# The last 256 gate and 256 up features of a feed-forward block as one more unit of seven block products, and its first two units taken by turns

## The chip, the cores and the metric

The kernel runs on one core of one Trainium2 chip. The metric is the device time of one launch in microseconds (us); smaller is better. Before the change the median of three runs is 862.22 us (861.01 to 862.43). One execution was also recorded by the hardware profiler, and everything below that is read from a view is read from that execution.

## The reference, cut to what matters

One encoder layer: two mixers, a cross-attention over a memory, and a feed-forward block (SwiGLU), on 512 tokens with 1024 features. The change is in the last block, and begins where the cross-attention ends:

```
h = h + memory_cross_attention(rms_norm(h, xattn_norm_g[i]), memn, w_q[i], w_k[i], w_v[i], w_xo[i])
h = h + swiglu(rms_norm(h, ffn_norm_g[i]), w_gate[i], w_up[i], w_down[i])
...
def swiglu(hn, w_gate, w_up, w_down):
    return (jax.nn.silu(hn @ w_gate) * (hn @ w_up)) @ w_down
```

`hn` is 512 x 1024, `w_gate` and `w_up` are 1024 x 2816, `w_down` is 2816 x 1024, all float32.

## The kernel before, in words

**Float32 from two halves.** TensorE is fed with operands that are split in two: `split` (line 83) casts a tile to a rounded half on ScalarE (line 85, "hi") and subtracts that from the tile on VectorE (line 86, "lo"). Each product of two such operands is three matmuls: hi by hi, hi by lo, lo by hi. So each block of weights that arrives from memory costs one cast on ScalarE and one subtraction on VectorE before TensorE may use it. The halves of weights live in three buffers each (`hi`, `lo`, line 108); a fourth block can be split only when the oldest of the three has been multiplied. Some blocks have a place of their own instead (`sums_place`, line 131: `s1`, `s2`, `s4`).

**Units of seven products.** 512 columns of `w_gate` or `w_up` are a unit. Its matrix product (two halves of the 1024 input features, two halves of the tokens, two halves of the columns) is done by Strassen's method in Winograd's form: seven block products in place of eight. They have the numbers 1, 2, 5, 6, 7, 4, 3 in the order of use. `product` (line 1252) does one: 24 matmuls with 256 moving columns. The weight side of 1, 2, 7 and 3 starts from blocks that are loaded as they are (tiles `b11`, `b21`, `b22`); that of 5, 6, 7 and 4 needs sums of blocks: `t` is loaded and a second block is added onto it by an accumulating DMA that GpSimd issues (line 193), and three further sums for each unit are made on VectorE (line 200). `plan_unit` (line 173) lists for each product its loads, how many products ahead each load is asked for (4 for `b11` and `b21`, 7 for `t`, 5 for the add onto `t` and for `b22`), and the making of its halves. `t`, `b21` and `b22` have two buffers each. The token side needs operands of its own: 1 and 2 take the tokens 0 to 255 as they are, 7 and 4 the tokens 256 to 511 or a difference, 5, 6 and 3 sums of both (`sum1`, `sum2`, `sum4`, lines 1729 to 1740).

**The last 512 columns are not a unit.** 2816 is five times 512 and 256 more. The last 256 columns of `w_gate` and of `w_up` (from `FS`, line 340) are multiplied in the ordinary way: `gate_part` (line 1767) and `feat` (line 1784), each 96 matmuls of 256 moving columns, thus four times the 24 of a product, eight for both. They go first, mixed with products 1 and 2 of the first unit, because the tokens 256 to 511 come out of the cross-attention and its norm later than the tokens 0 to 255 (`last_blocks`, line 1682; `turn_row`, line 1668). One matmul of 512 columns (`idle_product`, line 1265) writes to nothing that is read. Their results are `pair`: the gate part through SiLU on ScalarE (line 1717), then multiplied by the up part on VectorE (line 1720).

**What sets the order.** `plan` is the list of all blocks of weights in the order of their use. `next_w` (line 351) hands out the next one, asks for the loads that are due, and writes the splits of the next two blocks into the program. The program order is a priority only: a scheduler orders each engine's queue by it among what it takes to be ready, so that work written later stands earlier in a queue where nothing else was ready. `keep_in_program_order` and `behind` (line 117) pin single instructions. The queues are worked in that order on the chip. The copies and adds that prepare `w_down` (`plan_sums`, line 276) are hung on entries of the plan by their number, every fourth from entry 122 on (line 348): a copy that SyncE issues (line 293), and an accumulating DMA that GpSimd issues (line 294).

**Around it.** `unit_start` (1745) does product 1 and copies it, `unit_second` (1758) adds product 2 to the copy; the loop over the units is at line 1832, and in it products 1 and 2 of the next unit stand between the products of the present one.

Of the kernel before, what the change touches and what calls it, by code (L numbers as in the profile page):

```python
# [17 lines left out]
P = 128  # L18
# [34 lines left out]
def hybrid_layer_kernel(  # L53
# [29 lines left out]
    def split(dst_hi, dst_lo, src):  # L83

        hi = nc.scalar.copy(dst_hi, src)  # L85
        lo = nc.vector.tensor_tensor(dst_lo, src, dst_hi.bitcast(F32), ALU.subtract)  # L86
        if pinned[0]:
            in_order(hi)
            in_order(lo)
        return hi  # L90


    pinned = [False]
# [79 lines left out]
    def plan_unit(w, c0, ordered=False):  # L173

        kh = KD // 2
        b = lambda i, j: block(w, i * kh, kh, c0 + 256 * j, 256)
# [25 lines left out]
        def make(nm, *then):  # L202
# [6 lines left out]

        return {q: ((w, c0, q), loads, made) for q, loads, made in (  # L210
            (1, [(4, plain("b11", b(0, 0)))], make("b11")),
# [34 lines left out]
    def plan_units(units, down):  # L246


        made = [plan_unit(*u, ordered=i < 2) for i, u in enumerate(units)]
        for i in range(2):  # L250
            plan_block(w_gate, 4 * i, 4, FS, 256, place=i + 1, ordered=True,
                       then=None if i else lambda ins: behind(ins, xo_cast[0]))
            plan.append(made[0][i + 1])
        plan_feat(w_up, FS, KD)
        for i, m in enumerate(made):
# [85 lines left out]
    UNITS = [(w, c0) for c0 in range(0, FS, 512) for w in (w_gate, w_up)]  # L341
# [923 lines left out]
    def idle_product(x, y):  # L1265

        in_order(nc.tensor.matmul(aux("idle", (P, 2, 256)), x[:, 0, 0:P], y, start=True, stop=True))

# [372 lines left out]
    for wi in range(2):  # L1641
        held.append((wi,) + next_w(w_xo, 2 * wi, 2, 0, 512))
        for t in range(NT):
            out_rows(wi, t)
            tick(1.3)
            between.get((wi, t), lambda: None)()
    held += [(wi,) + next_w(w_xo, 2 * wi, 2, 0, 512) for wi in (2, 3)]
# [20 lines left out]
    def turn_row(t, turned=False):  # L1668
        to_feat(scaled.pop(t), fn_hi, fn_lo, slice(t * P, (t + 1) * P), full, turned=turned, copied=True)
# [46 lines left out]
    def gate_evac(m, j, ps):  # L1716
        nc.scalar.activation(pair[:, j, :], ps, AF.Silu)

    def up_evac(m, j, ps):
        nc.vector.tensor_tensor(pair[:, j, :], pair[:, j, :], ps, ALU.mult)  # L1720


    a11, a12, a21, a22 = full[:, K0, T0], full[:, K1, T0], full[:, K0, T1], full[:, K1, T1]
# [5 lines left out]
    def sum1():  # L1729
        V.tensor_tensor(a22, a21, a22, ALU.subtract)  # L1730
        make_op(5, 1, a22)

    def sum2():
        V.tensor_tensor(s3, a11, a21, ALU.subtract)
        V.tensor_tensor(a11, a22, a11, ALU.subtract)
        make_op(6, 2, a11)

    def sum4():
        V.tensor_tensor(a12, a12, a11, ALU.add)
        make_op(3, 4, a12)  # L1740

    fn_q = lambda ks, ts: (fn_hi[:, ks, ts], fn_lo[:, ks, ts])
    ops = {1: fn_q(K0, T0), 2: fn_q(K1, T0), 7: fn_q(K0, T1), 4: fn_q(K1, T1)}
# [7 lines left out]
    def put(u, f, ts, src):  # L1751
        dst = acts(u[1] // 512, f)[:, :, ts]
        if u[0] is w_gate:
            nc.scalar.activation(dst, src, AF.Silu)
# [6 lines left out]

    ps = [bank("pf0"), bank("pf1")]
    ws = []

    def gate_part(i, ts):
        if ts is T0:
            ws.append((4 * i,) + next_w(w_gate, 4 * i, 4, FS, 256))
        feat_block(ps, ws[i], fn, KD, 4, ts, ts is T0)  # L1770
        tick(2.7)

    gate_part(0, T0)
    begun = unit_start(UNITS[0])
    gate_part(1, T0)
    idle_product(ops[1][0], fn_hi[:, 4:6, T0])
    unit_second(UNITS[0], begun[1])
    for i in range(2):
        gate_part(i, T1)
    for j in range(2):  # L1780
        gate_evac(FS // P + j, j, ps[j])
    sum1()
    later(1, sum2)
    feat(w_up, FS, fn, KD, up_evac, parts=2, ps=[aux("pf0"), aux("pf1")])
# [246 lines left out]
```

## Time and profile before

| | |
|---|---|
| median of three runs | 862.22 us (861.01 to 862.43) |
| the profiled execution: span from first to last instruction (the page gives no other time for it) | 859.5 us |
| TensorE busy | 852.2 us |
| VectorE busy | 663.7 us |
| ScalarE busy | 465.9 us |
| GpSimd busy | 86.2 us |
| moved by DMA | 170.61 MB, mean 198 GB/s |

Times in the views are us from the start of the span. PE is TensorE, PEld its loading of the stationary operand, DVE is VectorE, ACT is ScalarE, POOL is GpSimd, SP is SyncE; a "q" behind a name is the issuing of DMAs. In the timeline a line has its start, its length, engine, program line, operation, output and inputs, and in square brackets the time for which the engine had been idle and what ended that. In the chain of waits a line has the start, the time it adds to the chain, engine, output, line and number of instructions.

### The profile page before, as it was taken

Reading aid. Unit: us, or ns where it says so; the run is one execution under the profiler, and the core shown is the slowest. Engines: PE = TensorE matmul, PEld = TensorE weight load, DVE = VectorE, ACT = ScalarE, POOL = GpSimd, SP = SyncE. Lnnn points to the kernel's source line nnn. Section 1 sums busy time; section 2 is a strip of 40 time slices with the busy share of each in tenths; the row PEclk is TensorE's granted clock in tenths of the full one; section 3 lists DMA queues with packets and bytes.
Section 4 is the critical chain, followed back from the end, with each engine's and each line's share of the span. In section 5 each row is a group of like instructions: output and inputs, shape, how many; then the busy total and the mean of one; then the engine's idle time right before and its main releaser. Section 6 shows DMA issues by size and latency. Waiting matters only on the chain.

```text
span 859.5 us, 14730 instructions
## 1 busy us (share of the span) xinstructions
PE 852.2 (99%) x5760; PEld 764.1 (89%) x5760; DVE 663.7 (77%) x1078; ACT 465.9 (54%) x698; POOL 86.2 (10%) x119
## 2 busy tenths in 40 slices
PE   9999999999999999999999999999999999999997
PEld 6888888888889988899899888999999999988886
DVE  7898898899646867678758656767877768899776
ACT  7834953244455534457557444645545554655674
POOL 0002101211021111010010001010211111000000
PEclk9999999999999999999999999999999999999999
DMA  9869666888575798635696555557899898366664
GB/s 270 229 229 252 143 171 160 227 212 203 138 221 162 250 321 260 213 110 196 215 275 169 133 152 143 147 176 180 206 242 234 209 230 219 96 186 203 200 192 164
DMA packets 116200, 170.61 MB, mean 198 GB/s; under 512 B 9489, under 2 KB 80801, under 8 KB 116002
## 3 DMA queue, kind: packets, MB, share of 16 engines
q1 hardware_dynamic: 95778, 140.51, 50.8%
q0 software_dynamic: 20064, 28.55, 20.3%
q8 instruction: 45, 0.74, 0.3%
q10 hardware_dynamic: 288, 0.61, 0.2%
q14 instruction: 25, 0.20, 0.1%
HBM read 160.75 MB, written 48.73 MB: 244 GB/s over the span
## 4 chain that ended last, share of the span: by engine, by line
PE 98%; DMA 1%; ACT 0%; SPq 0%; DVE 0%; issue 0%
PE pf L379 27%; PE pt L379 17%; PE px L1261 13%; PE pq L1261 6%; PE dx L379 5%; PE dq L379 5%; PE pv L1261 3%; PE bx L1261 3%; PE qx L1261 3%; PE dv L379 2%; PE pz L968 2%; PE qv L1261 1%; PE po L379 1%; PE psc L379 1%; PE py L1025 1%; PE qq L1261 1%
## 5 line engine op out<-in xcount | busy, mean ns | idle before, releaser
L85 ACT CAST whi<-wraw 128x1024 fp32r<-128x1024 f32 x141 | 145.3, 1031 | 161.4 <-PE pf L379 61.0
L86 DVE TENSOR_TENSOR wlo<-wraw,whi 128x1024 fp32r<-128x1024 f32 x141 | 168.2, 1195 | 55.5 <-ACT whi L85 54.8
L379 PE MATMUL pf<-xn,whi 128*128 128x512 f32 x448 | 139.4, 392 | 0.0
L379 PEld LDWEIGHTS pf<-xn,whi 128*128 128x128 f32 x448 | 83.4, 188 | 16.9 <-issue 0.2
L379 PE MATMUL pf<-xn,wlo 128*128 128x512 f32 x224 | 87.7, 392 | 0.0
L1261 PE MATMUL px<-fn,whi 128*128 128x256 f32 x480 | 83.5, 277 | 0.0
L1261 PEld LDWEIGHTS px<-fn,whi 128*128 128x128 f32 x480 | 72.5, 188 | 0.2
L86 DVE TENSOR_TENSOR wlo<-b,whi 128x1024 fp32r<-128x1024 f32 x40 | 48.9, 1223 | 26.0 <-ACT whi L85 26.0
L85 ACT CAST whi<-b 128x1024 fp32r<-128x1024 f32 x40 | 42.2, 1054 | 47.8 <-PE px L1261 27.8
L1261 PE MATMUL px<-fn,wlo 128*128 128x256 f32 x240 | 66.4, 277 | 0.0
L1261 PE MATMUL pq<-s,whi 128*128 128x256 f32 x320 | 55.0, 276 | 0.0
L86 DVE TENSOR_TENSOR wlo<-t,whi 128x1024 fp32r<-128x1024 f32 x30 | 36.7, 1225 | 19.4 <-ACT whi L85 19.4
L85 ACT CAST whi<-t 128x1024 fp32r<-128x1024 f32 x30 | 31.6, 1054 | 36.1 <-PE pv L1261 13.4
L379 PEld LDWEIGHTS pf<-xn,wlo 128*128 128x128 f32 x224 | 42.0, 188 | 8.9 <-issue 0.2
L1261 PEld LDWEIGHTS pq<-s,whi 128*128 128x128 f32 x320 | 48.1, 188 | 0.0
L1261 PEld LDWEIGHTS px<-fn,wlo 128*128 128x128 f32 x240 | 45.1, 188 | 0.0
L1261 PE MATMUL pq<-s,wlo 128*128 128x256 f32 x160 | 44.2, 276 | 0.0
L379 PE MATMUL pt<-whi,xn 128*128 128x512 f32 x128 | 43.4, 404 | 0.0
L379 PE MATMUL dx<-whi,s 128*128 128x512 f32 x132 | 41.4, 390 | 0.0
L379 PE MATMUL dq<-whi,s 128*128 128x512 f32 x122 | 38.1, 389 | 0.0
L294 POOL DMA_DIRECT2D dsum<-in_w_down_dram x12 | 13.3, 1105 | 170.4 <-DMA dsum<-in_w_down_dram 166.2
L1261 PEld LDWEIGHTS pq<-s,wlo 128*128 128x128 f32 x160 | 30.1, 188 | 0.0
(456 smaller groups left out, 2221.7 us busy)
## 6 DMA issues: line engine op xcount, KB each, us to landing
wraw<-in_w_in_dram SPq DMA_DIRECT2D x34, 512.0 KB, 5.2
dsum<-in_w_down_dram SPq DMA_DIRECT2D x20, 512.0 KB, 6.3
wraw<-dsum SPq DMA_DIRECT2D x20, 512.0 KB, 4.3
b<-in_w_gate_dram SPq DMA_DIRECT2D x15, 512.0 KB, 5.2
b<-in_w_up_dram SPq DMA_DIRECT2D x15, 512.0 KB, 5.4
wraw<-in_w_down_dram SPq DMA_DIRECT2D x15, 512.0 KB, 4.6
dsum<-in_w_down_dram POOLq DMA_DIRECT2D x10, 512.0 KB, 7.9
dsum<-dsum POOLq DMA_DIRECT2D x10, 512.0 KB, 7.9
```

The lines of the kernel that those rows point to most:

```text
L85: hi = nc.scalar.copy(dst_hi, src)
L86: lo = nc.vector.tensor_tensor(dst_lo, src, dst_hi.bitcast(F32), ALU.subtract)
L294: plan[j + step][1].append((0, lambda d=dst, x=more: nc.gpsimd.dma_start(d, x, accum_op=ALU.add)))
L379: m = nc.tensor.matmul(ps, a[x], b[y], start=start and i == 0, stop=stop and i == 2, skip_group_check=free)
L968: nc.tensor.matmul(ps[:, g, :], wt[:, g, :], u[:, o * GO + g, :], start=True, stop=True)
L1025: in_order(nc.tensor.matmul(ps[64 * j:64 * j + 64, :, :, h, :].rearrange("p q d c -> p d q c"), a, b, start=k == ks[0], stop=k == ks[2], t ...
L1261: nc.tensor.matmul(ps[:, j, :], a[x], b[y], start=start and j == k == i == 0, stop=k == 3 and i == 2, skip_group_check=True)
```

## The change

The 256 last columns of `w_gate` and the 256 last of `w_up` become one unit, number 0: its first half of columns is the gate part, its second the up part, done with the same seven products as the others. It has its results put into `pair`. The eight products' worth of ordinary matmuls and the idle matmul go.

The first stretch is now a list written out by hand, `LEAD`: a pair is (unit, product). Units 0 and 1 go by turns; products 1 and 2 of unit 2 stand among them. The ordinary loop starts with product 5 of unit 2. The token operands are made at other places: rows 256 to 511 are only copied to `full` when they have been transposed (`turn_row`), the operand of product 5 is made from them in two parts (`fifth_part`), then those of 6 (`sixth`), 7 (first `split_last`), 3 (`third`) and 4 (second `split_last`). A SiLU of one column (`ready`) is put at an earlier place, in the cross-attention's last stage. Units 0 to 2 have their loads in program order, before it was units 0 and 1. The diff, without the plain removal of `sum1`, `sum2`, `sum4`, `gate_evac`, `up_evac`, `gate_part` and `idle_product`:

```diff
-    def plan_unit(w, c0, ordered=False):
+    def plan_unit(w, c0, ordered=False, place=None):
...
-        b = lambda i, j: block(w, i * kh, kh, c0 + 256 * j, 256)
+        b = lambda i, j: block(w, i * kh, kh, c0 + 256 * j, 256) if c0 < FS or j == 0 else block(w_up, i * kh, kh, c0, 256)
...
+        def first():
+            ops = halves(r["b11"], place)
+            if place is not None:
+                behind(cast[0], xo_cast[0])
+            return ops
...
-            (1, [(4, plain("b11", b(0, 0)))], make("b11")),
+            (1, [(4, plain("b11", b(0, 0)))], first),
...
-        made = [plan_unit(*u, ordered=i < 2) for i, u in enumerate(units)]
-        for i in range(2):
-            plan_block(w_gate, 4 * i, 4, FS, 256, place=i + 1, ordered=True,
-                       then=None if i else lambda ins: behind(ins, xo_cast[0]))
-            plan.append(made[0][i + 1])
-        plan_feat(w_up, FS, KD)
-        for i, m in enumerate(made):
+        made = [plan_unit(*u, ordered=i < 3, place=None if i else 1) for i, u in enumerate(units)]
+        plan.extend(made[n][q] for n, q in LEAD)
+        for i, m in list(enumerate(made))[2:]:
...
-    UNITS = [(w, c0) for c0 in range(0, FS, 512) for w in (w_gate, w_up)]
+    UNITS = [(w_gate, FS)] + [(w, c0) for c0 in range(0, FS, 512) for w in (w_gate, w_up)]
+    LEAD = ((0, 1), (1, 1), (0, 2), (1, 2), (2, 1), (0, 5), (1, 5), (0, 6), (1, 6), (0, 7), (1, 7), (0, 4), (0, 3), (1, 4),
+            (2, 2), (1, 3))
...
+    ready = np_.tile([P, 1], F32, tag="ms", name="ready", bufs=2)
+    behind(nc.scalar.activation(ready, mhalf, AF.Silu), halved[0][0])
...
     def turn_row(t, turned=False):
-        to_feat(scaled.pop(t), fn_hi, fn_lo, slice(t * P, (t + 1) * P), full, turned=turned, copied=True)
+        if t < 2:
+            to_feat(scaled.pop(t), fn_hi, fn_lo, slice(t * P, (t + 1) * P), full, turned=turned, copied=True)
+            return
+        xs = scaled.pop(t)
+        for q in range(2):
+            ps = aux("ptr", (P, 4, P))
+            for j in range(4):
+                k = 4 * q + j
+                nc.tensor.transpose(ps[:, j, :], xs[:, k * P:(k + 1) * P], ident)
+            nc.scalar.copy(full[:, 4 * q:4 * q + 4, t * P:(t + 1) * P], ps)
...
+    def fifth_part(t):
+        if 5 not in ops:
+            ops[5] = sums_place(1, 4, 256, APART)
+        r = slice((t - 2) * P, (t - 1) * P)
+        V.tensor_tensor(s3[:, :, r], a21[:, :, r], a22[:, :, r], ALU.subtract)
+        split(ops[5][0][:, :, r], ops[5][1][:, :, r], s3[:, :, r])
+        fifth.extend(halved[0])
+        if t == 3:
+            behind(silus[0], fifth[-2])
+
+    def sixth():
+        V.tensor_tensor(a21, a11, a21, ALU.subtract)
+        behind(V.tensor_tensor(a11, s3, a11, ALU.subtract), fifth[-1])
         make_op(6, 2, a11)
+    def third():
         V.tensor_tensor(a12, a12, a11, ALU.add)
         make_op(3, 4, a12)
...
+    def lead_product(n, q):
+        u, d = UNITS[n], lead.setdefault(n, {})
+        if q == 1:
+            d["x"], d["v"] = unit_start(u)
+        elif q == 2:
+            unit_second(u, d["v"])
+        elif q == 5:
+            d["q"] = aux("pq").rearrange("p (j t) -> p j t", j=2)
+            product(d["q"], u, 5, True, ops)
+        elif q == 6:
+            product(d["x"], u, 6, False, ops)
+            d["u2"] = copied(d["x"], "u2")
+        elif q == 7:
+            product(d["x"], u, 7, False, ops)
+            d["u3"] = minus(d["q"], copied(d["x"], "u3"))
+            if n:
+                put(u, 1, T1, d["u3"])
+        elif q == 4:
+            product(d["x"], u, 4, False, ops)
+            put(u, 0, T1, d["x"])
+            if n == 0:
+                put(u, 1, T1, d["u3"])
+        else:
+            product(d["q"], u, 3, False, ops)
+            put(u, 1, T0, minus(d["q"], d["u2"]))
+
+    def split_last(ks, src):
+        behind(split(*fn_q(ks, T1), src), fifth[-2])
+
+    after = {(1, 1): lambda: fifth_part(2), (0, 2): lambda: fifth_part(3), (1, 2): sixth,
+             (2, 1): lambda: split_last(K0, a21), (0, 5): third, (0, 6): lambda: split_last(K1, a22)}
+    for n, q in LEAD:
+        lead_product(n, q)
+        after.get((n, q), lambda: None)()
+    begun = lead[2]["x"], lead[2]["v"]
...
-    for i, u in enumerate(UNITS):
+    for i, u in list(enumerate(UNITS))[2:]:
```

## The prediction on record

> **What bounds the kernel now.** I read the page first, then the chain of waits around the stretch that changes, then the timelines of single engines in it.
>
> ```profile
> span 859.5 us, 14730 instructions
> PE 852.2 (99%) x5760; PEld 764.1 (89%) x5760; DVE 663.7 (77%) x1078; ACT 465.9 (54%) x698; POOL 86.2 (10%) x119
> PEclk9999999999999999999999999999999999999999
> PE 98%; DMA 1%; ACT 0%; SPq 0%; DVE 0%; issue 0%
> ```
>
> The chain that ends last is TensorE for 98% of the span, and its clock is granted in full in each slice. A busy TensorE need not be one at its peak, so I look at how closely its instructions follow each other where the change is. The chain from the first feed-forward matmul on, with two gaps in the quotation:
>
> ```profile
> 534.17 0.24 PE pf L379 x2
> ...
> 538.05 0.44 PE ptr L539 x4
> 538.73 0.44 PE ptr L539 x4
> 541.71 0.44 PE ptr L539 x4
> 542.39 0.44 PE ptr L539 x4
> 544.36 0.23 PE idle L1267
> ...
> 547.31 16.32 PE pf L379 x144
> 563.63 2.72 PE pq L1261 x24
> ...
> 577.23 2.72 PE px L1261 x24
> 579.95 5.44 PE pq L1261 x48
> ```
>
> Each piece starts where the one before it ends; there is no wait in it. 144 matmuls take 16.32 us, 24 take 2.72 us: 0.1133 us for one of 256 columns, in the ordinary blocks and in the products alike. So here a matmul left out is worth 0.1133 us, as long as nothing else becomes late. What could is in the stages: the same stretch by engine, from the first feed-forward matmul to the last product of the first unit.
>
> ```profile
> 534.20:582.00 47.80, 47.80 (x421) 47.76 (x420) 36.54 (x40) 25.77 (x34) 4.35 (x4) 1.00 0.54 152
> ```
>
> TensorE is busy for all of 47.80 us, VectorE for 36.54, ScalarE for 25.77; the DMA engines have a share of 0.54. VectorE has 11.3 us to spare, and is the nearest.
>
> **What goes.** The 192 ordinary matmuls are eight times 24, the new unit is seven times 24: one product, 2.72 us. The idle matmul is 0.23 us. Transposes stay (four pieces of 0.44, 1.76 us). On TensorE the change is worth 2.95 us, all on the path.
>
> **What is added.** On ScalarE seven casts of weights in place of four and three copies and two SiLUs of results in place of two SiLUs: some six instructions, none over 1.1 us, against 22 us to spare in the window's row; nothing by itself. The first SiLU's table load moves out of the stretch:
>
> ```profile
> 548.31 1.28 ACT L1754 ACT_TABLE_LOAD   x1
> 519.53 0.63 ACT L505 ACTIVATE sq<-h 128x512 f32<-128x512 f32 x1 [6.54 <-DVE h L1451]
> ```
>
> Its new place is in the last stage of the attention, where ScalarE waits for 6.54 us at one point; I cost it at nothing. Without that cover it would delay a cast by 1.28 us. The DMAs: four loads of blocks go, five come. The share of 0.54 holds one block more.
>
> The cost is on VectorE. Its rows in the stretch, and the two that fix when it can begin:
>
> ```profile
> 538.34 1.42 DVE L531 SCALAR_TENSOR_TENSOR xs<-h,r,g_f 128x512 f32<-128x512 f32 x2 [0.73 <-POOL r L516]
> 542.28 1.16 ACT L545 COPY full<-ptr 128x512 f32<-128x512 f32 x2
> 563.66 1.22 DVE L86 TENSOR_TENSOR fn<-s,fn 128x1024 fp32r<-128x1024 f32 x1
> 564.80 1.22 DVE L200 TENSOR_TENSOR t<-t,b 128x1024 f32<-128x1024 f32 x1
> 565.93 0.68 DVE L1720 TENSOR_TENSOR pair<-pair,pf 128x512 f32<-128x512 f32 x1
> 566.53 1.22 DVE L86 TENSOR_TENSOR wlo<-b,whi 128x1024 fp32r<-128x1024 f32 x1
> ```
>
> A full operation (1024 columns) lasts 1.22 us, but the next starts 1.14 after it (563.66, 564.80); a half one lasts 0.68 and the next starts 0.60 later. I count by 1.14 and 0.60. The new unit has three lower halves of weights more and three sums that ordinary blocks don't need: six full operations. It evacuates with four half operations in place of two. The token operands lose about as much as one full one (the halves of rows 256 to 511 are made once, not for some columns twice). In all some 6.9 us more, in a stretch that gets 2.95 us shorter: of 11.3 us to spare 1.5 are left. So the average nearly closes, and I go by what is due when.
>
> Product number n of the list (from 0) starts at 534.2 + 1.76 + 2.72 n if nothing is late. VectorE is done with the norm of the last row at 538.34 + 1.42 = 539.76. Row 3's columns are in place at 542.28 + 1.16 = 543.44; until then there is the half difference and the lower half of row 2 and the lower half of one block of weights: 0.60 + 0.60 + 1.14 = 2.34 of 3.68 us, 1.34 idle.
> - Before unit 0's product 7 (n = 9, 560.44) are due: six lower halves of weights ((2,1), 5, 5, 6, 6, 7), three sums of weights, three operations for the operand of 6, one for that of 7: 13 full, and four half ones for the operand of 5: 14.82 + 2.40 = 17.22. There are 20.68 - 1.34 = 19.34: 2.1 us over.
> - Before unit 0's product 3 (n = 12, 568.60): eight full ones more (three halves of weights, two sums, three for the operands of 4 and 3) and one half one: 26.94 in all. There are 28.84 - 1.34 = 27.50, and the last has to be finished, not only followed (0.08): 0.5 us over.
> - Before product 4 of unit 1 (n = 13, 571.32): two full more, 29.22 of 30.22: 1.0 over.
>
> So if VectorE does each thing in the order of need, TensorE waits for nothing; with one full operation out of that order it waits 1.14 - 0.5 = 0.6 us. That is the value I take: the halves of the next weights stand ahead of the token operands in the program order, but something ready is taken where a half isn't yet. The ends are 0 and 3.6 (first rival). Below nothing it can't go: TensorE has no wait in the stretch that could be won.
>
> The Trainium skill, page "VectorE: DVE Perf Modes", section "The DRAIN you can't avoid", says that the next operation of this engine doesn't start until the pipeline of the one before is empty. By it the counts above would go by 1.22 and 0.69: 21 full and 5 half operations, 29.07 against 27.50, a wait of 1.6 us. The rows 563.66 to 566.53 don't agree, since there each operation starts 0.08 us before the one ahead has ended; only if that overlap is lost between engines' waits does it come out this way: 862.22 - 2.95 + 1.6 = 860.9.
>
> **The sum.** 2.95 - 0.6 = 2.35 us less. From the profiled execution's span that is 859.5 to 857.15; the span lies 2.7 us under the median of the runs, and I carry the difference over: 862.22 - 2.35 = 859.9.
>
> **First rival: VectorE takes what is ready, not what is due.** It has been seen:
>
> ```profile
> 553.12 1.21 DVE L1734 TENSOR_TENSOR s<-full 128x1024 f32<-128x1024 f32 x1
> 555.63 1.23 DVE L1739 TENSOR_TENSOR full<-full 128x1024 f32<-128x1024 f32 x1
> 561.92 1.23 DVE L86 TENSOR_TENSOR wlo<-t,whi 128x1024 fp32r<-128x1024 f32 x1 [2.72 <-ACT whi L85]
> ```
>
> L1739 is written after product 7 of the first unit, and runs at 555.63, before the half for its product 6 at 561.92. There VectorE still idled 2.72 us afterwards, so it cost nothing; now it would. Five full operations are ready before unit 0's product 7 and not due for it: the lower half of the operand of 4, two operations for the operand of 3, one sum of weights of each unit. If all five go first: 5 x 1.14 - 2.1 = 3.6 us of waiting, at products 6 and 7 of units 0 and 1. 862.22 - 2.95 + 3.6 = 862.9, no difference that can be measured. Against it: a half is cast two products ahead, and while halves wait they come first.
>
> **Second rival, slower: the third unit's sum comes too late.** `t` has two buffers. Unit 2's load waits until the half of unit 0's product 4 is made. Before, from that product to product 5 of unit 2 there are nine products, 24.5 us; in the list there are five, 13.6.
>
> ```profile
> 565.29 0.56 SPq L293 DMA_DIRECT2D dsum<-in_w_down_dram  x1
> 572.80 1.23 DVE L86 TENSOR_TENSOR wlo<-t,whi 128x1024 fp32r<-128x1024 f32 x1 [1.50 <-ACT whi L85]
> 574.05 0.38 SPq L186 DMA_DIRECT2D t<-in_w_gate_dram  x1
> 576.86 1.17 POOL L294 DMA_DIRECT2D dsum<-in_w_down_dram  x1 [29.05 <-DMA dsum<-in_w_down_dram]
> 578.37 1.32 POOL L193 DMA_DIRECT2D t<-in_w_gate_dram  x1 [0.34 <-issue]
> 571.72 1.05 ACT L85 CAST whi<-t 128x1024 fp32r<-128x1024 f32 x1 [1.18 <-PE px L1261]
> t<-in_w_gate_dram POOLq DMA_DIRECT2D x5, 512.0 KB, 7.1
> ```
>
> The load is issued at 574.05, as the half ends (574.03), 3.2 us before product 4 starts (577.23): 16.8 us are there. The add follows 4.3 us later, lands after 7.1, cast and half take 2.3: 13.7. That fits. But GpSimd's queue has an add for `w_down` ahead of it, which waited for a copy issued at 565.29 until 576.86, 11.6 us. The copies hang on entries of the plan and come 10.9 us earlier by the change (eight products' time for four entries goes, seven for seven comes), so that such a copy can be issued beside the load. If its add stands first, the chain is 11.6 + 1.5 + 7.1 + 2.3 = 22.5, 5.7 too long: 862.22 - 2.95 + 5.7 = 865.0. It decides from the point at which the add onto `t` is issued more than 7.4 us after its load. What speaks against it is that the 11.6 us ran beside other loads, and that the wait is hidden where the add for `w_down` is put behind.
>
> A wait of 5.7 us at one place has a further price by the Trainium skill, page "TensorE: Matmul & The Clock Gate", section "HAM oscillation — how this bites in real kernels": TensorE gaps beyond some 3.4 us bring its clock to half. No slice of this trace shows a clock under 9 tenths, so it can't be checked here.
>
> **How the numbers follow.** The forecast has 0.46: the ledger closes by need, barely. The first rival has 0.31, the lost overlap 0.02, the second rival 0.21. A measurement of this kernel can tell about 0.2% from no change, 1.7 us. Faster by more (under 860.5) is the forecast, 0.46; within it lie the first rival and the lost overlap, 0.33; slower by more (over 863.9) is the second rival, 0.21. The forecast alone reaches from 859.3 (no wait) to 860.5. The range for 8 in 10 adds half a us below for the spread of the runs, 858.8, and reaches over the first rival into the second, 864.4.
>
> **What would show it.** In the profile after: 25 matmuls fewer; TensorE's pieces still 2.72 us each; VectorE with less than 2 us idle from 540 to 570. Right: the waits in the list add to less than 1.2 us. First rival: waits of TensorE on `wlo` at products 6 and 7 of units 0 and 1, with operations of `third` or `split_last` ahead of the halves. Second: one wait before product 5 of unit 2, with GpSimd waiting for `dsum` ahead of the add onto `t`. I am wrong altogether if waits arise in the attention's last rows, before the list begins, or if a product's matmuls no longer follow at 0.1133 us.

## The result, and the profile after

| | before | after |
|---|---|---|
| median | 861.68 us (861.01 to 862.43, 6 runs) | 868.36 us (864.04 to 872.68, 6 runs) |
| profiled execution | span 859.5 us | 865.61 us, span 863.8 us |

The ratio is 1.0077, 95% interval 1.0052 to 1.0103: slower by 6.7 us, where 2.3 less was forecast, and outside the range. The runs of the kernel before lie within 1.4 us, those after within 8.6; this spread is a clue that the profile of one execution can't show. The page of the profile after:

```profile
span 863.8 us, 14699 instructions
PE 852.0 (99%) x5735; PEld 763.1 (88%) x5735; DVE 669.8 (78%) x1085; ACT 468.5 (54%) x703; POOL 87.4 (10%) x120
PE 95%; DVE 2%; DMA 1%; issue 1%; SPq 0%; ACT 0%
```

25 matmuls fewer (5760 to 5735), and still the same busy time, 852.0 us for 852.2. The chain has lost 3% of TensorE to VectorE and issue. TensorE's timeline, after, where it had been idle in the list of the first products; in brackets the idle time and what ended it. Before, there was none:

```profile
554.76 0.38 PE L1266 MATMUL pq<-s,wlo 128*128 128x256 f32 x1 [1.37 <-DVE wlo L86]
558.17 0.38 PE L1266 MATMUL px<-s,wlo 128*128 128x256 f32 x1 [0.51 <-DVE wlo L86]
561.58 0.50 PE L1266 MATMUL px<-s,whi 128*128 128x256 f32 x2 [0.63 <-ACT whi L85]
563.01 0.50 PE L1266 MATMUL px<-fn,whi 128*128 128x256 f32 x2 [0.93 <-ACT u L1780]
563.85 0.39 PE L1266 MATMUL px<-s,wlo 128*128 128x256 f32 x1 [0.34 <-DVE wlo L86]
```

Five waits, 3.78 us; from start to start, with the refilling of TensorE, these steps are 4.6 us longer than 0.1133 us each. They begin at product 5 of unit 1. VectorE's timeline shows what stood ahead of the half for it:

```profile
548.95 1.22 DVE L201 TENSOR_TENSOR t<-t,b 128x1024 f32<-128x1024 f32 x1
550.09 2.35 DVE L86 TENSOR_TENSOR fn<-full,fn 128x1024 fp32r<-128x1024 f32 x2
552.36 1.22 DVE L1755 TENSOR_TENSOR full<-full 128x1024 f32<-128x1024 f32 x1
553.49 1.22 DVE L86 TENSOR_TENSOR wlo<-t,whi 128x1024 fp32r<-128x1024 f32 x1
```

Both operand halves of `split_last` (2.35 us for two) and the sum of `third` run before the half at 553.49 that TensorE waits for until 554.76; none of the three is used before product 7. That is the first rival's order. The windows of the same stretch, with TensorE's busy time and instructions first and its clock third from the end:

```profile
553.00:560.70 7.70, 5.82 (x49) 5.42 (x47) 7.70 (x8) 1.27 (x2) 0.00 (x0) 1.00 0.00 0
560.70:564.40 3.70, 1.80 (x11) 1.20 (x10) 3.70 (x4) 3.20 (x4) 0.00 (x0) 1.00 0.00 0
564.40:567.70 3.30, 3.30 (x18) 3.30 (x17) 2.80 (x3) 0.00 (x0) 0.00 (x0) 0.50 0.46 108
```

VectorE is busy without a gap, TensorE only for 1.80 of 3.70 us, and then the clock is granted at 0.50 for 3.4 us, in which 18 matmuls are recorded; the distances of the starts make this 1.6 us. From the list's first matmul to the first one for `w_down` it is 210.1 us, before it was 206.3. -2.95 + 4.6 + 1.6 gives 3.25 of the 3.8 us; a further 0.5 arose before the list, and 0.5 I can't assign. Behind the half clock each product takes 2.72 us, as before. This profiled execution is shorter than the median, though (865.61 for 868.36). What the longest ones lose is not in it.

### The profile page after: what moved, and what is told of

Its sections match the earlier page's. It is cut to its first block, busy times and chain, and to the rows that moved or that the text cites. A ratio compares the mean times of both kernels' runs of the same rounds, so it can differ in the third digit from the quotient of the medians.

```text
span 863.8 us, 14699 instructions
## 1 busy us (share of the span) xinstructions
PE 852.0 (99%) x5735; PEld 763.1 (88%) x5735; DVE 669.8 (78%) x1085; ACT 468.5 (54%) x703; POOL 87.4 (10%) x120
## 4 chain that ended last, share of the span: by engine, by line
PE 95%; DVE 2%; DMA 1%; issue 1%; SPq 0%; ACT 0%
PE pf L384 24%; PE pt L384 17%; PE px L1266 13%; PE pq L1266 6%; PE dx L384 5%; PE dq L384 5%; PE pv L1266 3%; PE bx L1266 3%; PE qx L1266 3%; PE dv L384 2%; PE pz L973 2%; PE qv L1266 1%; PE po L384 1%; PE psc L384 1%; PE py L1030 1%; PE qq L1266 1%
## 5 line engine op out<-in xcount | busy, mean ns | idle before, releaser
L85 ACT CAST whi<-wraw 128x1024 fp32r<-128x1024 f32 (+1 forms) x139 | 143.2, 1030 | 163.0 <-PE pf L384 62.3
L86 DVE TENSOR_TENSOR wlo<-wraw,whi 128x1024 fp32r<-128x1024 f32 (+1 forms) x139 | 165.9, 1195 | 55.8 <-ACT whi L85 54.8
L1266 PE MATMUL px<-fn,whi 128*128 128x256 f32 x512 | 89.1, 277 | 0.9 <-ACT u L1780 0.9
L1266 PEld LDWEIGHTS px<-fn,whi 128*128 128x128 f32 x512 | 77.3, 188 | 1.3 <-ACT u L1780 1.1
L1266 PE MATMUL px<-fn,wlo 128*128 128x256 f32 x256 | 70.7, 276 | 0.0
L1266 PE MATMUL pq<-s,whi 128*128 128x256 f32 x352 | 60.6, 276 | 0.0
L86 DVE TENSOR_TENSOR wlo<-t,whi 128x1024 fp32r<-128x1024 f32 x33 | 40.4, 1224 | 18.4 <-ACT whi L85 18.4
L1266 PEld LDWEIGHTS pq<-s,whi 128*128 128x128 f32 x352 | 53.0, 188 | 0.0
L1266 PE MATMUL pq<-s,wlo 128*128 128x256 f32 x176 | 48.7, 277 | 1.4 <-DVE wlo L86 1.4
L1266 PE MATMUL px<-s,whi 128*128 128x256 f32 x176 | 32.7, 285 | 0.6 <-ACT whi L85 0.6
```

What stands on the lines that cost most here:

```text
L1266: nc.tensor.matmul(ps[:, j, :], a[x], b[y], start=start and j == k == i == 0, stop=k == 3 and i == 2, skip_group_check=True)
```

## The experiments

The kernel before ran beside each group of runs on the same chip: 861.55 us beside the first four; 861.20 beside the idle matmul left out, the 24 matmuls left out alone, and the idle matmul put back (alone and with VectorE's order); 861.43 beside the late idle matmul, the queue on GpSimd, all repairs and the first move of product 1; 861.46 beside the idle matmul of 256 columns and the two runs with the earlier load; 861.61 beside the last two. Units count from 0 in the code; in words unit 0 is the first unit, unit 2 the third.

### The list: order on VectorE, third sum, or fewer matmuls

The kernel after once more, unaltered:

> The changed kernel once more, unaltered, for a second profile and more times: its six runs lie between 864.0 and 872.7 us, those of before between 861.0 and 862.4. If the loss is VectorE's order alone (4.8 us of TensorE waiting in the list and one stretch at half clock, 1.7 us), the second profile shows the same waits, and the times can't spread by 8 us, since an engine's order is fixed. If the third unit's sum by DMA comes late in some runs, a slower profile shows a wait of TensorE before product 5 of unit 2 that the first one did not have, and the spread is there. If the throttle makes the spread, the slower profile has more stretches at half clock, 1.7 us each.

867.44 us (865.42 to 872.60, 6 runs), ratio 1.0080 (1.0053 to 1.0107): the same loss and the same spread, so that VectorE's order alone is not all of it. Its profile has the same waits in the list, the half clock, and a wait that the first didn't have, before the list, in the attention's last rows:

```profile
526.10 1.10 PE L544 MATMUL ptr<-ident,xs 128*128 128x128 f32 x6 [1.75 <-DVE xs L536]
```

Then the order on VectorE. `recs` keeps the halves of each entry of the plan; operations not yet due are put behind halves that are:

```diff
-            nc.vector.tensor_tensor(r[o], r[x], r[y], op)
+            return nc.vector.tensor_tensor(r[o], r[x], r[y], op)
...
-                    tt(*then)
+                    ins = tt(*then)
+                    if ordered:
+                        behind(ins, halved[0][1])
...
-        V.tensor_tensor(a12, a12, a11, ALU.add)
+        behind(V.tensor_tensor(a12, a12, a11, ALU.add), recs[lead0 + 10][1])
...
-    def split_last(ks, src):
+    def split_last(ks, src, n):
         behind(split(*fn_q(ks, T1), src), fifth[-2])
+        behind(halved[0][1], recs[lead0 + n][1])
...
-             (2, 1): lambda: split_last(K0, a21), (0, 5): third, (0, 6): lambda: split_last(K1, a22)}
+             (0, 5): lambda: split_last(K0, a21, 7), (1, 6): lambda: (split_last(K1, a22, 10), third())}
```

> The changed kernel, with five groups of VectorE operations pinned behind the halves of weights that are due first (both last halves of the token operands, the sum for operand 3, the two sums of weights of units 0 to 2). Nothing is left out. If VectorE's order is the cause, TensorE's waits in the list fall from 4.8 us to under 1.5 us, no stretch at half clock follows, and the span falls by 4 to 5 us, to about 859 to 860. If VectorE's work as such is too much, the waits only move to later products and the span stays within 1 us. If the third unit's sum is the limit, the waits in the list go, but a wait of 1 to 5 us appears before product 5 of unit 2, and the times still spread by several us.

868.60 us (862.10 to 872.15, 12 runs), ratio 1.0065 (1.0042 to 1.0088). In the profile (867.62 us) the waits in the list and the half clock are gone, so VectorE's order was their cause. Still the time isn't lower. The chain, with start, length and number of matmuls:

```profile
555.13 14.37 PE px L1272 x122
569.50 2.83 PE pq L1272 x24
...
577.75 2.84 PE pq L1272 x24
580.59 0.03 DVE wlo L86
580.62 1.10 issue
581.72 0.68 DVE a_up L1775
582.40 1.15 DVE t L201
...
584.60 1.05 ACT whi L85
585.66 0.04 issue
585.70 6.35 PE px L1272 x51
```

Two things are new. Behind 580.59 TensorE waits for the third unit's sum `t`, whose cast starts at 579.50, when the sum has landed, and then for the sum that VectorE makes from it (2.0 us from start to start, at products 5 and 6). And a product takes 2.83 us, not 2.72: 0.1178 us for a matmul, with nothing between them, at a clock of 1.000. But for some twenty matmuls behind that wait it stays so for all units, 7.6 us in sum.

Third, the kernel after without the add onto the third unit's `t`, which leaves that sum incomplete:

```diff
+                if w is w_up and c0 == 0:
+                    return
                 add = nc.gpsimd.dma_start(r[nm], src, accum_op=ALU.add)
```

> The changed kernel without the accumulating DMA onto t of unit 2: the second block isn't added, so that sum is left out of the result. VectorE's order stays. By the first theory the waits in the list stay (some 4.8 us), so the fastest times stay at 864 to 866 us. By the second the spread of 8 us goes, and all runs lie near the fastest of the changed kernel, 864; if the sum is not what spreads them, the runs still reach 870.

866.53 us, median of five with one outlier of 4909.87, which the ratio leaves out; ratio 1.0052 (1.0037 to 1.0066). The waits in the list are there as in the kernel after, so they don't come from that add. The other four runs lie between 865.01 and 867.09; four are too few to say that the times near 872 are gone without the add, or that the 1 us to the kernel after is its price.

Fourth, the other direction: the kernel before, without 24 matmuls of the gate part (for the tokens 256 to 511 the first half of the input features is left out of it) and without the idle matmul.

```diff
-    idle_product(ops[1][0], fn_hi[:, 4:6, T0])
...
-    for i in range(2):
-        gate_part(i, T1)
+    gate_part(1, T1)
```

> The kernel before, without 24 matmuls of the gate part of the last 256 columns (the first half of the input features for the tokens 256 to 511 is left out) and without the idle matmul: the change's share on TensorE alone. If a matmul left out is worth 0.1133 us there, the time falls by 2.95 us, to 858.7 from 861.7. If something else were waiting behind TensorE in that stretch, it falls by less than 2.

865.63 us (865.28 to 865.66), ratio 1.0044 (1.0032 to 1.0056). The 25 matmuls gone, no wait in the stage, and 4 us slower. In its profile each product takes 2.83 us, from the list to the last unit. That was not expected; the next three runs look for what sets this pace.

### The pace: the idle matmul

The kernel before, with only the idle matmul left out:

> The kernel before, with its one idle matmul of 512 columns (ahead of product 2 of the first gate unit) left out and nothing else; the output is the same. Pace theory: the idle matmul is what brings the matmuls of 256 columns back from 0.118 us to 0.113 us one after the other; without it each product takes 2.83 us, as in the run of before that lacked it together with 24 matmuls, for some 70 products, and the time is 861.6 + 7 to 8, so 868.5 to 869.5 us. Rival (by the prediction's sum a matmul left out is time gained): 861.3 us with products of 2.72 us; the slow pace of the other run then came from the 24 matmuls that it lacked, not from the idle one.

868.89 us (868.35 to 869.03), ratio 1.0086 (1.0073 to 1.0099): 7.7 us slower by one matmul less. The chain:

```profile
545.33 2.83 PE pv L1261 x24
...
564.53 2.83 PE pq L1261 x24
567.36 8.48 PE px L1261 x72
```

The kernel before without the 24 matmuls alone (the same part left out), the idle matmul kept:

> The kernel before without the 24 matmuls of the third gate block on the second half of the tokens (that part of the gate features is left out of the sum), with its idle matmul kept. Pace theory: the idle matmul holds the pace of 0.113 us, the 24 matmuls are worth what they took, 861.6 - 2.7 = 858.9 us. Rival, that the pace depends on what follows and not on the idle matmul: 865 to 866 us as in the run without both.

859.03 us (858.25 to 860.02), ratio 0.9973 (0.9962 to 0.9984). The median falls by 2.2 us. In the profile it is 203.54 us from the first product to `w_down`, for 206.26: 2.72 us, just what the 24 took. The chain:

```profile
544.75 0.23 PE idle L1267
544.97 2.73 PE pv L1261 x24
...
561.30 2.72 PE pq L1261 x24
```

And the kernel before with the idle matmul cut to 256 columns:

```diff
-        in_order(nc.tensor.matmul(aux("idle", (P, 2, 256)), x[:, 0, 0:P], y, start=True, stop=True))
+        in_order(nc.tensor.matmul(aux("idle", (P, 2, 256))[:, 0, :], x[:, 0, 0:P], y[:, 0, :], start=True, stop=True))
```

> The kernel before with its idle matmul at 256 columns in place of 512; the output is the same. If what restores the pace is the longer matmul: 0.118 us a matmul from there on, as without the idle matmul, 868.5 to 869.5 us. If any extra matmul at that place does it (one that writes another bank, or the shift by one in the order of the two banks): as before, 861.1 us.

868.46 us (868.22 to 871.53), ratio 1.0084 (1.0070 to 1.0099), as without it. The chain:

```profile
547.16 0.12 PE idle L1267
547.28 2.83 PE pv L1261 x24
...
567.06 2.83 PE pq L1261 x24
```

So a stream of 256-column matmuls runs at one of two paces, 0.1133 or 0.1178 us, and keeps the one it has while nothing else comes between; one matmul of 512 columns at this place brings back the faster, and one of 256 does not. Other breaks change it too: in the kernel before, 33 matmuls from 534.0 us on go at 0.118, 21 from 539.6 on, behind transposes, at 0.113, 11 from 542.9 on, behind the next ones, at 0.118, and from the idle matmul on all at 0.113. Nor is it the width alone: those 33 come straight behind 24 matmuls of 512 columns of the attention, and in all profiles the stage starts at 0.118 behind these.

### The idle matmul put back, early and late

The kernel after with the idle matmul behind product 2 of the first unit:

```diff
         lead_product(n, q)
+        if (n, q) == (0, 2):
+            idle_product(ops[1][0], fn_hi[:, 4:6, T0])
```

> The kernel after, with an idle matmul of 512 columns put back behind product 2 of the first unit. Pace theory: the matmuls run at 0.113 us from there on in every execution, so the runs at 870 and over are gone; the waits for VectorE in the interleaved list stay, some 4 to 5 us, so 863 to 865 us with a spread under 1 us. Rival, that the spread comes from the waits themselves or from the half clock behind them: 864 to 872 as before.

873.28 us (867.76 to 874.57), ratio 1.0121 (1.0096 to 1.0145). That falls: slower, and the spread is there. Its profile is of the longest execution (874.57 us). Behind the idle matmul the pace is 0.113 us, then come the waits in the list, and after them it is slow to the end of the units (two of the pieces):

```profile
578.58 2.83 PE pq L1266 x24
...
584.23 2.83 PE pv L1266 x24
```

Some 7 us in sum. After the same waits the profile of the kernel after has 0.113 us. So a stop can be followed by the one pace or by the other, which would give two groups of times, by execution: the clue from the result. (For the kernel after itself only executions of 865.61 and 867.95 us were profiled; that those near 872 us look so is concluded from this one.)

The same profile has the wait in the last rows at its largest, 2.16 us of idle time before `ptr` at 526.38. GpSimd's timeline there:

```profile
523.60 1.33 POOL L194 DMA_DIRECT2D t<-in_w_gate_dram  x1 [11.99 <-DMA t<-in_w_gate_dram]
524.42 1.12 POOL L521 TENSOR_TENSOR r<-ms,mhalf 128x1 f32<-128x1 f32 x1
```

The inverse root `r` for the first of the last four tiles of rows stands behind the issue of an add onto `t`, and that waits for its load to land. In the kernel before, the root stood first (at 520.79, the add at 521.38). The cause is in the code: only the first add is put `behind` a root (`powers.clear()` empties the list), and by the change a second one, for unit 1, is issued here.

The idle matmul at that place together with VectorE's order:

> The kernel after with the idle matmul put back and VectorE's operations kept behind the weight halves that are due first. Pace theory together with the order theory: no waits in the list, products at 2.72 us, so the 2.72 us of the 24 matmuls come through unless unit 2's sum is late: 859 us without that wait, up to 863 us with it (waits before products 5 and 6 of unit 2, as in the run with the order alone). If the order costs nothing and only the pace does: as the run with the idle matmul alone. If neither theory holds: 867 to 869 us as with the order alone.

869.09 us (863.91 to 873.19), ratio 1.0091 (1.0061 to 1.0120). No wait in the list; 0.113 us from 548 to 561 us, then a small stop, 0.118 from 567 on, and stops of 1.7 us at the third unit's sum. An idle matmul helps until the next stop.

So the next one goes behind the last of them, into the loop, behind product 6 of the third unit, in the kernel after:

```diff
         product(x, u, 6, False, ops)
+        if i == 2:
+            idle_product(ops[1][0], fn_hi[:, 4:6, T0])
```

> The kernel after with one idle matmul of 512 columns behind product 6 of the third unit, behind the last place where the profiles show TensorE waiting. Theory now: every stop of TensorE can leave the matmuls of 256 columns at 0.118 us, and only an idle matmul behind the last stop brings 0.113 us for the rest; then the whole stage from there on runs at 2.72 us a product in every execution, the runs near 870 and over are gone, and 863 to 867 us are left (4 to 5 us of waits in the list, 1.7 us of half clock, 0 to 4 us of the wait in the attention's last rows, less 2.7). Rival, that the idle matmul does not act there or that the spread has another cause: 864 to 873 us as before, with products of 2.83 us in the profile of a slow execution.

867.28 us (867.02 to 869.90, 6 runs), ratio 1.0068 (1.0051 to 1.0084). No time is over 870, and the spread is 2.9 us in place of 8.6, as the theory had it. That is weak evidence: of twelve executions of the kernel after, four were over 870, so that six without one can be luck. In this profile the pace is 0.113 us already from 568.3 on, ahead of the idle matmul, so it doesn't show it at work. The times lie at and above the upper end of what was expected; the waits in the list, the half clock and 1.0 us (from start to start) in the last rows stay.

The queue on GpSimd alone:

```diff
-                    behind(add, powers[-NT])
-                    powers.clear()
+                    behind(add, powers[1 - NT])
```

> The kernel after with the adds onto the sums of the first three units kept, on GpSimd's queue, behind the inverse root of the second of the last four rows. Theory: the wait of TensorE for the turned rows (2.16 us in the run with the idle matmul behind product 2, 1.8 us in the first repeat) comes from the inverse root queued behind an add that waits for its load; it is gone here, and with it up to 2.2 us and the half clock behind it; waits in the list and the pace as in the kernel after: two groups of times, 863.5 to 866 and 869 to 871 us. Rival, that the rows wait for something else: a wait of 1 to 2 us there in the profile.

865.35 us (864.30 to 871.50, 8 runs), ratio 1.0053 (1.0029 to 1.0078), in two groups, 864.3 to 865.7 and 870.8 to 871.5. The wait in the rows is gone from the profile:

```profile
524.73 0.55 POOL L520 TENSOR_TENSOR r<-ms,mhalf 128x1 f32<-128x1 f32 x1 [3.39 <-DVE ms L519]
525.33 1.34 POOL L194 DMA_DIRECT2D t<-in_w_up_dram  x1
```

### All repairs together, and the third unit's sum

VectorE's order, the queue on GpSimd, and both idle matmuls:

> The kernel after with all repairs: VectorE's operations behind the weight halves that are due, the adds behind the second row's inverse root, and an idle matmul both behind product 2 of the first unit and behind product 6 of the third. If the causes found (order on VectorE, pace, GpSimd's queue, half clock) are all of the loss, the 2.72 us of the change come through, less the wait of the third unit's product 5 for its sum, 0 to 2.5 us: 859 to 861.5 us. If one cause is still missing: 863 us or more.

862.35 us (861.44 to 865.66, 12 runs), ratio 1.0011 (1.0000 to 1.0022). 5.8 of the 6.7 us are back, and the time lies between the two that were expected. What is left is seen in the chain of its profile (the longest execution, 865.66 us):

```profile
572.51 9.80 DMA t<-in_w_up_dram
...
582.39 1.05 ACT whi L85
583.45 0.02 issue
583.47 1.24 DVE wlo L86
584.71 0.04 issue
584.75 4.39 PE pq L1271 x22
589.14 3.06 PE px L1271 x26
592.20 0.23 PE idle L1277
592.43 5.22 PE px L1271 x46
```

The add onto the third unit's `t` takes 9.80 us to land, and product 5 waits for cast and half behind it. The last three lines show the late idle matmul at work: 0.1177 us a matmul ahead of it, 0.1135 behind.

Product 1 of the fourth unit moved ahead of products 5 and 6 of the third, so that the sum has 2.7 us more:

```diff
-            plan.extend([m[5], m[6]] + between + [m[7], nx[2] if nx else down[1], m[4], m[3]])
+            plan.extend((between + [m[5], m[6]] if i == 2 else [m[5], m[6]] + between) + [m[7], nx[2] if nx else down[1], m[4], m[3]])
...
+        if i == 2:
+            begun = unit_start(UNITS[3])
         q = unit_bank("pq")
         product(q, u, 5, True, ops)
...
-        if not final:
+        if i == 2:
+            pass
+        elif not final:
             begun = unit_start(UNITS[i + 1])
```

> As the kernel with all repairs, and the fourth unit's product 1 goes ahead of the third unit's products 5 and 6, so that the third unit's sum has 2.7 us more. If that sum is what is still late, the waits before products 5 and 6 of the third unit go: 858.8 to 859.8 us, and faster than the kernel before. If the sum is not late, the same time as the kernel with all repairs within 0.5 us.

862.92 us (860.45 to 867.92), ratio 1.0011 (0.9996 to 1.0025). The wait at the sum is gone from the profile, but a new one of 1.0 us stands behind it: two matmuls of the fourth unit's product 5 had been put early into TensorE's queue.

The other way, the load of that sum earlier: the half of the first unit's product 4, which frees the buffer, ahead of `split_last` and `third`. (The pins that keep product 3's operand ahead of what follows are not shown.)

```diff
-        behind(V.tensor_tensor(a12, a12, a11, ALU.add), recs[lead0 + 10][1])
+        behind(V.tensor_tensor(a12, a12, a11, ALU.add), recs[lead0 + 11][1])
...
-             (0, 5): lambda: split_last(K0, a21, 7), (1, 6): lambda: (split_last(K1, a22, 10), third())}
+             (0, 5): lambda: split_last(K0, a21, 7), (0, 7): lambda: (split_last(K1, a22, 11), third())}
```

> The kernel with all repairs, with VectorE's half of the first unit's weights for product 4 ahead of the second operand half and the third sum (behind them in the run before, where the half ended at 568.28 us and the load of the third unit's sum was issued at 568.31, as it freed the buffer), so that this load is issued some 2.3 us earlier. If the third unit's sum is the rest of what is lost (862.35 us against 859.2 for all 24 matmuls less two idle ones), the wait of 1 to 2 us before product 5 of the third unit goes and the time is 860 to 861 us. If the load is not what is late: 862 to 862.5 us, with the wait still there.

861.62 us (859.57 to 863.50, 11 runs), ratio 0.9997 (0.9986 to 1.0008), again between the two. The load is issued at 565.27 in place of 568.31, but takes 6.32 us to land in place of 3.63, and the three loads behind it, two of them issued 3 us earlier as well, land at most 1 us earlier. So the add is issued only 0.4 us earlier (572.15 for 572.51), and lands at 580.5 in place of 582.3; the list itself began 0.8 us earlier. The DMA engines' share is 0.84 from 565 to 572 us here, and was 1.10 from 572.5 to 582.3 with all repairs; that they had no room for more is likely, but not shown. Waits of 0.2 and 0.6 us are left at products 5 and 6 of the third unit, and a new one of 0.9 us stands at 574.30, for a block whose load landed at 573.11. A third idle matmul behind product 7 of the first unit:

> As the kernel with the earlier half, with a third idle matmul behind product 7 of the first unit, since the profile with two shows products of 2.83 us between 562 us and the second idle matmul at 592. It costs 0.23 us and is worth 0.11 us a product for up to ten products: 0.3 to 0.9 us faster than the run beside it, if small stops after it do not bring the slow pace back; if they do, 0.2 us slower.

861.39 us (859.70 to 863.26), ratio 0.9996 (0.9987 to 1.0006): not to be told from the run beside it.

At last both: the earlier load and product 1 of the fourth unit ahead, its product 5 kept behind the third's product 3.

> The kernel with the earlier half and two idle matmuls, with the fourth unit's product 1 ahead of the third unit's products 5 and 6 (2.7 us more for the third unit's sum), and the fourth unit's product 5 kept behind the third's product 3, which the first run of this order had two matmuls too early (1.3 us there). If the third unit's sum is the rest of what is lost (861.6 against 859.2): no wait over 0.5 us before products 5 and 6 of the third unit, and 859.2 to 860.5 us, faster than the kernel before by 1 to 2 us. If the time stays at 861 to 862: the rest is elsewhere.

862.63 us (861.65 to 864.29), ratio 1.0012 (1.0003 to 1.0021), 1 us slower than with the earlier load alone on another chip. No wait for the sum in the chain, but there is another one:

```profile
592.32 2.62 PE px L1276 x23
594.94 0.02 issue
594.96 1.04 ACT whi L85
596.00 0.49 ACT u L1798
596.50 0.04 issue
596.54 3.00 PE px L1276 x24
```

Product 4 needs the copy `u` of its bank, which stands on ScalarE behind a cast; the product that had covered this was the one moved ahead. So the sum was late, and its relief costs as much elsewhere (1.5 us of idle time here). With the third idle matmul:

> As the run beside it with the third idle matmul behind product 7 of the first unit: 0 to 0.3 us faster than the run beside it by the pair measured before (861.39 against 861.62), so 859 to 860.3 us; if the idle matmul costs more than the pace it saves, 0.2 us slower.

862.62 us (861.65 to 865.82), ratio 1.0010 (1.0001 to 1.0019): the same. None of the versions beats the kernel before.

## Why the prediction was wrong

- **The first step that failed: "one full operation out of that order", 0.6 us of waits, "the value I take".** The waits in the list measured 4.6 us, and 1.6 us of half clock came behind them: this is what the profiled execution lost. VectorE's order is the cause: with it pinned, no wait in the list and no half clock is left. All twelve timed executions of the kernel after took 864.04 us or more.
- **The second: "The idle matmul is 0.23 us", "a matmul left out is worth 0.1133 us".** Its place was read as a cost. Leaving it out of the kernel before, alone, costs 7.7 us (861.20 to 868.89). The prediction read the pace only behind it, at 547.31 and later. Its quotation of the chain has more gaps than the two that it names, and the lines that could have warned are in them:

```profile
534.52 2.59 PE pf L379 x22
...
542.83 1.53 PE pf L379 x13
...
544.59 2.73 PE pv L1261 x24
```

  The first two are at 0.1177 us a matmul, the third, behind the idle matmul, at 0.1138. The prediction had named a pace other than 0.1133 us as what would make it wrong altogether, and gave it no chance. What this step cost the kernel after is shown less well: both of its profiles have 0.113 us behind the waits, and the idle matmul put back alone gave 873.28 us, no gain. The time came back with VectorE's order, GpSimd's queue and two idle matmuls together; whether it needs the early one of the two was not tested.
- **24 matmuls, 2.72 us:** right, to the hundredth in the profile, where the idle matmul is kept and nothing becomes late.
- **VectorE's ledger:** by need it closes: with VectorE's order pinned the profile has no wait in the list, at products of 2.83 us, and with the idle matmul too only small stops near 561 us. But the forecast's 0.6 us of waits supposed an order near to need; the scheduler's was the first rival's.
- **The first rival (0.31):** right in its mechanism. Its price was 3.6 us, measured are 4.6, and 1.6 for the half clock behind it, which it did not have; the waits begin one product earlier than it said, at product 5 of unit 1. By these sizes it gives 862.22 - 2.95 + 4.6 = 863.9, and 865.5 with the half clock, which is the faster end of the kernel after.
- **The lost overlap (0.02):** it did not come. In the kernel after, full operations of VectorE still follow each other at 1.14 us (548.95, 550.09). The passage that the prediction quotes from the Trainium skill, page "VectorE: DVE Perf Modes", section "The DRAIN you can't avoid", goes on to say that a next operation which is not held starts earlier. These rows agree with that.
- **The second rival (0.21):** the sum `t` of unit 2 is late as soon as the list has no waits (2.0 us in the run with the order alone). Not through an add for `w_down` ahead on GpSimd, as it had it; the add onto `t` itself takes 8.3 to 9.8 us in the five profiles that wait for it at product 5, where 7.1, the median of the trace before, had been taken. In the kernel after, the list's own waits hid it.
- **"The DMAs: four loads of blocks go, five come":** priced by DMA share alone. The queue that one of them stands in was not followed: GpSimd's, ahead of the inverse root, for stops of 1.0 to 2.3 us (from start to start) in the last rows of the attention in four of the profiles. And the share at one place was double the mean: 1.10 where the third unit's sum is loaded, in the profile with all repairs.
- **SiLU's table load at nothing:** it is at 500.79 us now, and no engine waits for it. With VectorE's order alone pinned, nothing in the list waits for ScalarE.
- **The clock.** The prediction left the price of a long wait to the Trainium skill, page "TensorE: Matmul & The Clock Gate", section "HAM oscillation — how this bites in real kernels", which speaks of gaps beyond 3.4 us. One such gap is in its trace after all, at the end: TensorE's last matmul ends at 853.97 us, and the clock is at half from 858.44 on, as that section has it. But the runs also show that no single gap of that length is needed. Before the end of the kernel no idle time of TensorE was over 2.2 us, and the clock was halved in seven profiles all the same, once each. In the windows of 3.41 us just ahead, TensorE was busy for 1.56 us (after), 1.29 (the idle matmul put back) and 1.21 (all repairs). A low sum in such a window goes with it, though not by a sharp limit.

The balance of the 6.7 us is thus: -2.7 for the matmuls; the list 4.0 to 4.6 and the half clock 1.6; 0 to 2.3 in the last rows; and 0 or some 7 for the pace, by execution, the last one concluded and not shown for the kernel after. Not settled is what in the machine holds the two paces, and what decides which one follows a stop. In all five profiles with a half clock behind the list's waits (the kernel after twice, without the add, with the late idle matmul, with GpSimd's queue) the pace behind it is 0.113 us, and in the one with these waits and no half clock there (the idle matmul put back) it is 0.118; but behind the half clock with all repairs it was 0.118 too, so that this alone doesn't decide it.

## What to carry to other kernels

Before an instruction is taken out because nothing reads it, take out that one alone and look at the distance of those behind it; in a long stream of equal matmuls a difference of 4% in each is worth more than the whole edit, and an idle longer matmul belongs behind the last place where the stream can stop (three profiles show it at work there, at 592.0, 590.2 and 589.3 us). An order that closes by need holds only if it is pinned, since the queue is filled by what is ready. A load that is added is priced by who stands behind it in its queue, and by the DMA engines' share at that place, not by the mean share.

## What the runs showed of the hardware

- Matmuls of 256 columns, stationary side loaded for each, follow each other at 0.1133 or 0.1178 us at the full clock, for up to some 200 us. Behind a single one of 512 columns among them they went at the first in all nineteen places, thirteen of which had the second ahead; one of 256 didn't bring that (one run). Straight behind a row of 24 of 512 columns they went at the second in every profile. Transposes and stops can lead to either.
- Before the end of a kernel the half clock lasts 3413 ns each time (from 564.4 to 567.8 us in the kernel after). Counted in steps of this length, windows with 0.35 to 0.57 of TensorE busy were followed by it, others, away from the kernel's first and last us, with 0.51 to 0.64 were not.
- An accumulating DMA of 512 KB, the add onto the third unit's `t`, took 6.1 to 9.8 us to land. A load issued 3 us earlier into a busy stretch took 6.32 us in place of 3.63, so that the add behind it was issued only 0.4 us earlier.
